# Two-layer decoder trunk on one core: scores a head further ahead, norm factors spread by matmuls, two tiles divided anew

## The chip, the core and the metric

The kernel runs on one core of a Trainium2 chip. The metric is the time of one execution on the device in microseconds (us); a version's time is the median of several executions. A difference under 0.2% (2.8 us here) is treated as no difference.

## The reference

`h` is 512 tokens by 1024 channels, all in float32. Two layers are computed, each an attention, a SwiGLU feed-forward part and a gated embedding:

```python
# layer 0: stick-breaking attention, 16 heads of 64
q, k, v = split(rms(h) @ sb_w_qkv)                 # 1024 -> 3 x 1024
z = q @ k.T * 64**-0.5
later = reverse_cumsum(where(strict, -softplus(z), 0)) - where(strict, -softplus(z), 0)
w = where(strict, exp(log_sigmoid(z) + later), 0)
h += (w @ v) @ sb_w_o
# layer 1: softmax attention with a forget bias, keys and values from the shared projection
kvf = rms(h, shared_norm_g) @ shared_w_kvf         # keys, values, 16 forget logits a token
f_cum = cumsum(log_sigmoid(kvf[..., 2048:] + b_f), over tokens)
h += softmax(rms(q) @ rms(k).T * 64**-0.5 + f_cum[q] - f_cum[k]) @ v @ fox_w_o
# every layer, then
h += (silu(rms(h) @ w_g) * (rms(h) @ w_u)) @ w_d   # 2816 wide
h += sigmoid(rms(h) @ ple_w_gate) * (p[i] @ ple_w_proj)
```

## The kernel before

`h` is held channels by tokens: 8 tiles `h0` to `h7` of 128 channels by 512 tokens. Every product keeps float32 accuracy by splitting both operands into a high part (`wh`, `bh`: rounded by ScalarE) and a rest (`wl`, `bl`: subtracted by VectorE), and by three matmuls, high by high, high by rest and rest by high. `dense` makes one 128 by 512 output tile so (three matmuls for each of 8 input tiles); `by_token` makes its output tokens by channels, with 256 columns a matmul. Weights come as units of 128 by 1024, in the order of use, into two buffers `raw` by DMAs on SP's queue; `load_unit` splits a unit into `wh` and `wl`, three units ahead of use.

The norms' row factors are not applied to `h` but after the product. `norm_sums` sums squares by four small matmuls (tile `ssq`) and makes the 4 columns `r` with a Newton iteration on VectorE. The factors are needed along the free dimension too, in tile `rb` (128 by 512, equal rows): `norm_spread` makes it by four matmuls against the identity into tile `pb` and a ScalarE copy, `norm_bounce` by writing `r` to DRAM (`row<-r`) and reading it back to all partitions (`rb<-row`), both on SP's queue.

An attention interleaves three streams by hand. `front(hd)` makes the scores of a head in three PSUM tiles `z` (512, 384 and 256+128 columns) and turns them into weights `w`: in layer 0 ScalarE takes two sigmoids `e` and `w`, VectorE runs a product scan over `e` (L630) and multiplies (L633). `back(hd)` turns `w` by TensorE transposes in three groups (`pt`, L682: 4, 4 and 2 blocks, two PSUM buffers in turn), splits each group into high and rest (`w3h`/`w3l`, `w2h`/`w2l`, `w1h`/`w1l`), multiplies them with the values into `po` (L690), and adds the two halves into `at` (ScalarE L710, VectorE L711). `fill` holds other work for TensorE between these steps: keys and queries of later pairs of heads (`qk`: `kr`, then `ke`/`kd` and `qd`, of which halves are copied across partitions by DMAs that GpSimd issues, L518), values, and part of the output product. `STEPS[layer]` is the order in which one head's steps are taken: "f" is a step of the next head's `front`, "g" one of this head's `back`, and the number says how many steps of `fill` follow. A scheduler then moves instructions within each engine's queue; every queue runs in order.

In layer 1 the queries and keys are made by token in groups of four heads (`group`), with a norm a head (L551 to L565, result `qn`), and turned by `expand` (tile `qt`, L586). At the start of the layer, `group(0, sums, gates)` makes the queries, calls `sums` (which calls `norm_sums` and `norm_bounce`), and the rest of `forget` (L474 on) needs `rb` for the forget logits `zf`, whose running sum goes through DRAM (`gdram`) to the tiles `gb` that the scores need.

The gated embedding at the end of each layer (in `ffn`) makes for each tile `n` a gate product `pg` (24 matmuls) and a projection `pp` (6), then `gate` computes `h += sigmoid(pg * rb) * pp`. Its last tile is done in two parts of 384 and 128 columns (`LASTS`).

Of the kernel before, what the change touches and what calls it, by code (L numbers as in the profile page):

```python
# [18 lines left out]
F32 = mybir.dt.float32  # L19
# [5 lines left out]
P = 128  # L25
# [4 lines left out]
NP = 8  # L30
EPS = 1e-6
EXPLN = "natural_log_exp_and_others"
LASTS = [(0, 384), (384, 128)]
FULL = [(0, 512)]


# [49 lines left out]
def trunk(ctx, tc, xT, pT, small, wf, wall, out, dump=None):  # L86
# [8 lines left out]


    sm = const.tile([P, NG], F32, name="sm")
    nc.sync.dma_start(sm, small)
    h = []
    for k in range(ND):  # L100
        h.append(res.tile([P, S], F32, name=f"h{k}", tag=f"h{k}"))
    ident = const.tile([P, P], F32, name="ident")
    make_identity(nc, ident)

# [21 lines left out]
        nc.vector.tensor_tensor(out, a, b.bitcast(F32), ALU.subtract)  # L126


    raws, units = {}, {}
    gains = {}  # L130
    state = {"unit": 0, "block": 0, "low": "vector"}
    NU = wall.shape[0]
# [5 lines left out]
    def load_unit(u):  # L138
# [5 lines left out]
        if u in gains:  # L144
            c0, nk = gains[u]
            n = 1024 // nk
            for k in range(nk):
                c, g = slice(k * n, (k + 1) * n), sm[:, c0 + k:c0 + k + 1]
                nc.scalar.activation(wh[:, c], raw[:, c], AF.Copy, scale=g)
                nc.vector.scalar_tensor_tensor(wl[:, c], raw[:, c], g, wh[:, c].bitcast(F32),  # L150
                                               ALU.mult, ALU.subtract)
        else:
            nc.scalar.copy(wh, raw)  # L153
            if state["low"] == "dma":

# [109 lines left out]
    def dense(*args):  # L265
        return run(dense_steps(*args))
# [8 lines left out]
    def ffn(layer, buf, g_next):  # L275
        last = layer == 1
        with tc.tile_pool(name=f"pf{layer}", bufs=8, space=PSUM, reuse_waits="tile") as ppool["d"], \
# [44 lines left out]
            dumph(f"h_ffn{layer}")  # L322

            px = [(ph[:, k, :], pl[:, k, :]) for k in range(2)]
            tiles = [(n, 0, S) for n in range(ND)]
            tiles[-1:] = [(ND - 1, c0, cn) for c0, cn in LASTS]

            def gate():
                n, c0, cn, pp, pg = waiting.pop(0)
                s = ft.tile([P, S], F32, name="s", tag="s")  # L330
                nc.vector.tensor_tensor(s[:, :cn], pg[:, :cn], rb[:, c0:c0 + cn], ALU.mult)
                nc.scalar.activation(s[:, :cn], s[:, :cn], AF.Sigmoid)
                nc.vector.tensor_tensor(s[:, :cn], s[:, :cn], pp[:, :cn], ALU.mult)
                grow(n, s, c0, cn)
                if last:
                    nc.sync.dma_start(out[:, n * S + c0:n * S + c0 + cn], h[n][:, c0:c0 + cn])
                else:
                    emit_x(n, 1 - buf, g_next, True, c0, cn)

            blocks = [take(10) for n in range(ND)]  # L340
            for i, (n, c0, cn) in enumerate(tiles):
                if i == 0:
                    pp = dense(blocks[n], px, c0, cn)
                pg = dense(blocks[n] + 2, xs, c0, cn)
                if i > 0:
                    pp = dense(blocks[n], px, c0, cn)
                waiting.append((n, c0, cn, pp, pg))
                if i == 0:
                    m, r = norm_sums()
                elif i == 1:  # L350
# [13 lines left out]
    def attention(layer, buf):  # L364
# [3 lines left out]
        with tc.tile_pool(name=f"pa{layer}", bufs=1, space=PSUM, reuse_waits="tile") as pa, \  # L368
# [12 lines left out]
            vq = {}  # L381
            tok = {}

            def by_token(xs, emit, halves=((0,), (1,))):

                b = take(16)
                for hs in halves:
                    pss = {t2: ppool["d"].tile([P, 2, 256], F32, name="psv", tag="d") for t2 in hs}
# [153 lines left out]
            def group(g, before=None, after=None):  # L542

                for what in "qk":
# [24 lines left out]
                    if what == "q" and before is not None:  # L569
# [2 lines left out]
                        before()  # L572
                        for a in held:
                            emit(*a)
                        run(after)
                    else:
                        yield from by_token(xs, emit)
                    if what == "q":
# [141 lines left out]
            else:  # L720
                def sums():
# [1 line left out]

                    tok["em"] = a1.tile([P, 4], F32, name="em")
                    nc.vector.tensor_scalar_mul(tok["em"], m, EPS)
                    tok["rb"] = norm_bounce(tok["r"])
                    next(gates)

                gates = forget()
# [11 lines left out]
                    grow(n, ps)  # L741
                    yield

            run(front(0))
            with (tc.manual_schedule(engines={mybir.EngineType.PE}) if PIN[layer] else nullcontext()):
                for hd in range(NH):
                    if hd == 2 * WO_SPLIT:
                        fill.add("wo", first_part())
                    if hd + 1 < NH:
                        fill.finish(f"{'p' if stick else 'e'}{(hd + 1) // 2}")  # L750
                        f = front(hd + 1)
                    else:
                        f = iter(())
                    if hd % 4 == 0:
# [36 lines left out]
    for k in range(ND):  # L791
        nc.sync.dma_start(h[k], xT[:, k * S:(k + 1) * S])
        if k in (0, 4):
            fetch(k // 4)
    for k in range(ND):
        emit_x(k, 0, G_ATTN[0], False)
        if k in (0, 4):
# [135 lines left out]
```

## Time and profile before

| | us |
|---|---|
| median of 3 executions (lowest, highest) | 1397.88 (1397.15, 1398.16) |
| the profiled execution: its own time | 1396.51 |
| the profiled execution: its span, first to last instruction | 1394.7 |
| TensorE busy in the span | 1359.7 (97%) |
| VectorE busy in the span | 807.2 (58%) |
| ScalarE busy in the span | 633.3 (45%) |

A share of busy time is an average over stages. Matmuls overlap: one of 512 columns is shown as some 0.39 us long while the next starts 0.227 us after it, so a wait of TensorE costs more than the gap that the profile shows. The stages, by the first and last instruction: loads 0 to 7, first values and keys 7 to 50, first attention's heads 50 to 283 (from the first score to the sums of squares), feed-forward part and embedding to 701, second attention to 985, the rest of layer 1 to 1394.7.

### The profile page before, as it was taken

The numbers are of one execution on the slowest core, as the hardware profiler recorded it, in microseconds if no ns is written. First come the engines' busy times: TensorE is split into PE (matmuls) and PEld (weight loads), VectorE is DVE, ScalarE is ACT, GpSimd is POOL, SyncE is SP. The second block draws the span as 40 slices with busy tenths as digits, with TensorE's granted clock in tenths as the row PEclk, the third lists the DMA queues.
The fourth block names the chain that finished last, engine by engine and source line by source line (L and its number), as shares of the span: only waits on it lengthen the run. The fifth ranks groups of instructions, "written<-read, shape, count | busy, mean of one in ns | idle before, by whom it ended". The sixth has DMA issues, their size and how long they took to land.

```text
span 1394.7 us, 18219 instructions
## 1 busy us (share of the span) xinstructions
PE 1359.7 (97%) x7108; PEld 1147.6 (82%) x7108; DVE 807.2 (58%) x1396; ACT 633.3 (45%) x1114; POOL 45.4 (3%) x96
## 2 busy tenths in 40 slices
PE   7999999999999999999969999999999999999999
PEld 7778877788888888888968999987888888888887
DVE  6788888844444443334847788778454444433335
ACT  5566666623332332222547888767333233322312
POOL 0110010000000000000001101100000000000000
PEclk9999999999999999999999999999999999999999
DMA  5332232333333333232254333332333332323323
GB/s 182 104 93 77 69 99 61 92 84 116 95 91 106 91 104 93 91 106 68 91 70 137 93 98 91 99 106 76 84 119 93 98 99 91 106 91 101 95 68 106
DMA packets 41958, 133.71 MB, mean 96 GB/s; under 512 B 7936, under 2 KB 8320, under 8 KB 41872
## 3 DMA queue, kind: packets, MB, share of 16 engines
q1 hardware_dynamic: 37488, 119.92, 29.8%
q0 software_dynamic: 4384, 12.62, 3.4%
q8 instruction: 56, 0.92, 0.3%
q14 instruction: 30, 0.25, 0.1%
HBM read 121.99 MB, written 2.14 MB: 89 GB/s over the span
## 4 chain that ended last, share of the span: by engine, by line
PE 83%; DVE 5%; ACT 5%; issue 4%; DMA 2%; POOL 0%; SPq 0%; DVEq 0%; POOLq 0%; ACTq 0%
PE ps L251 23%; PE ps L252 23%; PE ps L253 23%; PE psv L399 3%; PE psv L398 3%; PE psv L400 3%; PE po L690 2%; PE pt L682 2%; PE z L597 1%; DVE e L630 1%; PE z L598 1%; ACT ke L506 1%; DMA row<-r 1%; DVE w L633 1%; ACT qd L506 1%
## 5 line engine op out<-in xcount | busy, mean ns | idle before, releaser
L251 PE MATMUL ps<-bh,wh 128*128 128x512 f32 (+1 forms) x1232 | 483.7, 393 | 1.4 <-ACT bh L713 1.4
L252 PE MATMUL ps<-bl,wh 128*128 128x512 f32 (+1 forms) x1232 | 478.4, 388 | 0.0
L253 PE MATMUL ps<-bh,wl 128*128 128x512 f32 (+1 forms) x1232 | 478.1, 388 | 0.0
L153 ACT CAST wh<-raw 128x1024 fp32r<-128x1024 f32 x192 | 202.0, 1053 | 471.9 <-PE ps L252 414.6
L126 DVE TENSOR_TENSOR wl<-raw,wh 128x1024 fp32r<-128x1024 f32 x192 | 234.6, 1222 | 160.6 <-ACT wh L153 160.0
L253 PEld LDWEIGHTS ps<-bh,wl 128*128 128x128 f32 x1232 | 231.4, 188 | 46.6 <-DVE wl L126 0.2
L251 PEld LDWEIGHTS ps<-bh,wh 128*128 128x128 f32 x1232 | 231.8, 188 | 44.9 <-ACT bh L713 1.8
L252 PEld LDWEIGHTS ps<-bl,wh 128*128 128x128 f32 x1232 | 231.8, 188 | 43.6 <-DVE bl L126 0.4
L398 PE MATMUL psv<-wh,bh 128*128 128x256 f32 x512 | 151.4, 296 | 9.8 <-ACT wh L153 7.0
L399 PE MATMUL psv<-wl,bh 128*128 128x256 f32 x512 | 147.5, 288 | 0.5 <-DVE wl L126 0.5
L400 PE MATMUL psv<-wh,bl 128*128 128x256 f32 x512 | 147.4, 288 | 0.0
L398 PEld LDWEIGHTS psv<-wh,bh 128*128 128x128 f32 x512 | 99.5, 195 | 10.4 <-ACT wh L153 7.0
L294 DVE TENSOR_TENSOR s<-s,ps 128x512 f32<-128x512 f32 x44 | 30.3, 688 | 124.5 <-PE ps L253 124.3
L399 PEld LDWEIGHTS psv<-wl,bh 128*128 128x128 f32 x512 | 99.5, 194 | 1.7 <-DVE wl L126 0.8
L400 PEld LDWEIGHTS psv<-wh,bl 128*128 128x128 f32 x512 | 99.4, 194 | 0.1
L251 PE MATMUL ps<-eh,wh 128*128 128x512 f32 x224 | 87.1, 389 | 0.0
L252 PE MATMUL ps<-el,wh 128*128 128x512 f32 x224 | 87.1, 389 | 0.0
L253 PE MATMUL ps<-eh,wl 128*128 128x512 f32 x224 | 87.1, 389 | 0.0
L292 DVE TENSOR_TENSOR s<-ps,rb 128x512 f32<-128x512 f32 x44 | 30.2, 691 | 97.9 <-PE ps L253 79.9
L682 PE MATMUL pt<-ident,w 128*128 128x128 f32 x320 | 52.5, 275 | 6.4 <-DVE w3l L126 5.4
L630 DVE TENSOR_TENSOR_SCAN e<-e 128x512 f32<-128x512 f32 (+1 forms) x64 | 50.2, 812 | 3.2 <-ACT e L627 2.9
L682 PEld LDWEIGHTS pt<-ident,w 128*128 128x128 f32 x320 | 38.0, 140 | 16.7 <-DVE w3l L126 10.2
(142 smaller groups left out, 1567.1 us busy)
## 6 DMA issues: line engine op xcount, KB each, us to landing
raw<-in_w_dram SPq DMA_DIRECT2D x216, 512.0 KB, 3.6
kd<-ke POOLq DMA_DIRECT2D x32, 128.0 KB, 3.3
ke<-kd POOLq DMA_DIRECT2D x32, 128.0 KB, 4.2
gb<-gdram POOLq DMA_DIRECT2D x16, 256.0 KB, 3.7
h<-in_x_dram SPq DMA_DIRECT2D x8, 256.0 KB, 5.9
out_dram<-h SPq DMA_DIRECT2D x7, 256.0 KB, 2.0
rb<-row SPq DMA_DIRECT2D x5, 256.0 KB, 4.5
pf<-in_p_dram SPq DMA_DIRECT2D x2, 512.0 KB, 3.7
```

The costliest lines, as they stand in the source:

```text
L126: nc.vector.tensor_tensor(out, a, b.bitcast(F32), ALU.subtract)
L153: nc.scalar.copy(wh, raw)
L251: nc.tensor.matmul(ps, wh, xh, start=first, stop=False)
L252: nc.tensor.matmul(ps, wh, xl, start=False, stop=False)
L253: nc.tensor.matmul(ps, wl, xh, start=False, stop=last)
L292: nc.vector.tensor_tensor(s, g, rb, ALU.mult)
L294: nc.vector.tensor_tensor(s, s, u, ALU.mult)
L398: nc.tensor.matmul(ps[:, st], xh, wh, start=first, stop=False)
L399: nc.tensor.matmul(ps[:, st], xh, wl, start=False, stop=False)
L400: nc.tensor.matmul(ps[:, st], xl, wh, start=False, stop=lastk)
L630: nc.vector.tensor_tensor_scan(e[:, c:c + m], e[:, c:c + m], e[:, c:c + m], 1.0, ALU.mult, ALU.bypass)
L682: nc.tensor.transpose(pt[:, bi * P:(bi + 1) * P], blk(j, s), ident)
```

## The change

In layer 0, `front` runs two heads ahead of `back` instead of one (`LEAD`), with nine instead of six buffers for `w` and a new order of steps, in which the scores' three steps are spread between those of `back`. In layer 1's attention, `rb` is made by `norm_spread` within the first group's key product instead of by `norm_bounce`, and that product's first tile takes the PSUM bank of `qt` (tile `k0`). In both layers the last embedding tile keeps its gate product whole and divides only the projection, into halves of 256. The first weight unit is loaded and split as 256 and 768 columns, and `h0` is loaded first.

```diff
-LASTS = [(0, 384), (384, 128)]
+HALVES = [(0, 256), (256, 256)]
...
-    nc.sync.dma_start(sm, small)
+    nc.sync.dma_start(h[0], xT[:, :S])
+    raw0 = wpool.tile([P, 1024], F32, name="raw0", tag="raw", bufs=2)
+    nc.sync.dma_start(raw0[:, :256], wall[0, :, :256])
+    nc.sync.dma_start(sm, small)
+    nc.sync.dma_start(raw0[:, 256:], wall[0, :, 256:])
...
+        elif u == 0:
+            for c in (slice(0, 256), slice(256, 1024)):
+                nc.scalar.copy(wh[:, c], raw[:, c])
+                minus(wl[:, c], raw[:, c], wh[:, c])
...
             def gate():
-                n, c0, cn, pp, pg = waiting.pop(0)
+                n, pp, pg = waiting.pop(0)
                 s = ft.tile([P, S], F32, name="s", tag="s")
-                nc.vector.tensor_tensor(s[:, :cn], pg[:, :cn], rb[:, c0:c0 + cn], ALU.mult)
-                nc.scalar.activation(s[:, :cn], s[:, :cn], AF.Sigmoid)
-                nc.vector.tensor_tensor(s[:, :cn], s[:, :cn], pp[:, :cn], ALU.mult)
-                grow(n, s, c0, cn)
...
+                nc.vector.tensor_tensor(s, pg, rb, ALU.mult)
+                nc.scalar.activation(s, s, AF.Sigmoid)
+                for c0, ps in pp:
+                    c = slice(c0, c0 + S // len(pp))
+                    nc.vector.tensor_tensor(s[:, c], s[:, c], ps[:, :S // len(pp)], ALU.mult)
+                    nc.vector.tensor_tensor(h[n][:, c], h[n][:, c], s[:, c], ALU.add)
+                    if last:
+                        nc.sync.dma_start(out[:, n * S + c0:n * S + c0 + S // len(pp)], h[n][:, c])
...
+                elif n:
+                    pp = [(c0, dense(blocks[n], px, c0, cn)) for c0, cn in HALVES]
...
+                    elif after is not None:
+                        steps = by_token(xs, emit, first_bank=lambda: pz.tile(
+                            [P, S], F32, name="k0", tag="n", bufs=1))
+                        for _ in range(ND - 1):
+                            yield next(steps)
+                        tok["rb"] = norm_spread(tok["r"], pz, "z")
                         run(after)
+                        yield from steps
...
-                    tok["rb"] = norm_bounce(tok["r"])
...
-            run(front(0))
+            for hd in range(LEAD[layer]):
+                run(front(hd))
...
-                    if hd + 1 < NH:
-                        fill.finish(f"{'p' if stick else 'e'}{(hd + 1) // 2}")
-                        f = front(hd + 1)
+                    nxt = hd + LEAD[layer]
+                    if nxt < NH:
+                        fill.finish(f"{'p' if stick else 'e'}{nxt // 2}")
+                        f = front(nxt)
...
-WB = (6, 4)
+WB = (9, 4)
+LEAD = (2, 1)
...
-    [("f", 1), ("f", 1), ("f", 2), ("g", 2), ("g", 1), ("g", 1), ("g", 1), ("g", 2), ("g", 1)],
+    [("g", 1), ("f", 1), ("g", 1), ("g", 1), ("f", 2), ("g", 1), ("g", 2), ("f", 1), ("g", 2)],
```

What this does to the queues is seen in the order of the built instructions. First TensorE in a head in the middle of layer 0's attention, from the first transposes `pt` to the third group (the dense matmuls `ps` between them cut). Before:

```order
L682 MATMUL pt<-ident,w 128x128 x4
L251 MATMUL ps<-bh_104,wh_1706 128x512
L252 MATMUL ps<-bl_106,wh_1706 128x512
L253 MATMUL ps<-bh_104,wl_1707 128x512
...
L682 MATMUL pt<-ident,w 128x128 x4
...
L690 MATMUL po<-w3h,v 128x512
...
L682 MATMUL pt<-ident,w 128x128 x2
```

And in the changed kernel (line numbers there are its own: L682 is now L707, L597 is L622):

```order
L707 MATMUL pt<-ident,w 128x128 x4
...
L622 MATMUL z<-ke,qd 128x512
L623 MATMUL z<-kd,qd 128x512
...
L707 MATMUL pt<-ident,w 128x128 x4
...
L715 MATMUL po<-w3h,v 128x512
...
L622 MATMUL z<-ke,qd 128x384
L623 MATMUL z<-kd,qd 128x384
...
L707 MATMUL pt<-ident,w 128x128 x2
```

Between the first and the third group, which use the same PSUM buffer, stood 12 dense matmuls, one group of transposes and one product; now 18 dense matmuls and two score tiles stand there beside them. Before, all scores of the next head stood ahead of the first group.

Second, VectorE at the start of the heads of layer 0's attention, from the second head's middle score tile on (`kr` is the next pair's keys, `kd` their rest). Before:

```order
L630 SCALAR_TENSOR_TENSOR e<-e 128x384
L633 TENSOR_TENSOR w<-w,e 128x383
L126 TENSOR_TENSOR w3l<-pt,w3h 128x512
L630 SCALAR_TENSOR_TENSOR e<-e 128x256
L630 SCALAR_TENSOR_TENSOR e<-e 128x128
L633 TENSOR_TENSOR w<-w,e 128x255
L633 TENSOR_TENSOR w<-w,e 128x127
L126 TENSOR_TENSOR w2l<-pt,w2h 128x512
L535 TENSOR_TENSOR kr<-ps,rb 128x512
L126 TENSOR_TENSOR w1l<-pt,w1h 128x256
L126 TENSOR_TENSOR wl_695<-raw_692,wh_694 128x1024
L508 SCALAR_TENSOR_TENSOR kd<-kr,ke 64x512 x2
```

And in the changed kernel:

```order
L655 SCALAR_TENSOR_TENSOR e<-e 128x384
L658 TENSOR_TENSOR w<-w,e 128x383
L553 TENSOR_TENSOR kr<-ps,rb 128x512
L655 SCALAR_TENSOR_TENSOR e<-e 128x256
L655 SCALAR_TENSOR_TENSOR e<-e 128x128
L658 TENSOR_TENSOR w<-w,e 128x255
L658 TENSOR_TENSOR w<-w,e 128x127
L130 TENSOR_TENSOR wl_676<-raw_673,wh_675 128x1024
L526 SCALAR_TENSOR_TENSOR kd<-kr,ke 64x512 x2
```

`kd` and what follows from it now come ahead of the first head's `w3l`, `w2l` and `w1l`. On TensorE the third head's first score, which needs `kd`, has moved forward: 44 dense matmuls stand between the first head's first score and it, where 47 and all products of the first head stood.

Third, ScalarE in layer 1 behind the forget logits' product `fps`. Before:

```order
L471 COPY zf<-fps 16x512
L551 ACTIVATE sqn<-psv 128x512
L477 ACTIVATE ef<-zf 16x512
L560 ACTIVATE r_5844<-mm 128x8
L478 ACTIVATE ef<-ef 16x512
```

And in the changed kernel:

```order
L489 COPY zf<-fps 16x512
L247 COPY rb<-pb 128x512
L569 ACTIVATE sqn<-k_5725 128x512
L495 ACTIVATE ef<-zf 16x512
L496 ACTIVATE ef<-ef 16x512
```

The copy of `pb` is new here. On TensorE the four matmuls into `pb` stand behind the first 42 of the 48 matmuls into `k0`, and on SP's queue the two DMAs of `norm_bounce` are gone.

## Rows read from the trace of the kernel before

**Rows 1.** Busy time by stretch: stretch, its length, busy us (instructions) by engine, clock, DMA.
```profile
0.00:7.05 7.05, 0.00 (x1) 0.01 (x1) 0.99 (x4) 3.57 (x4) 1.77 (x12) 1.00 0.67 196
...
50.40:70.70 20.30, 18.09 (x90) 13.50 (x91) 17.87 (x28) 13.51 (x26) 2.07 (x4) 1.00 0.32 80
70.70:239.10 168.40, 164.04 (x942) 133.92 (x943) 141.97 (x225) 110.99 (x213) 12.36 (x24) 1.00 0.28 79
239.10:283.10 44.00, 43.12 (x205) 34.42 (x204) 35.15 (x51) 26.18 (x43) 0.00 (x0) 1.00 0.31 94
...
700.90:744.30 43.40, 30.10 (x223) 27.42 (x222) 21.95 (x68) 17.07 (x42) 3.71 (x7) 0.88 0.53 91
```

**Rows 2.** TensorE's groups by line and shape, 70.7 to 239.1 us.
```profile
L251 PE MATMUL ps<-bh,wh 128*128 128x512 f32 x120 | 51.9, 433 | 0.0
...
L682 PE MATMUL pt<-ident,w 128*128 128x128 f32 x129 | 20.9, 275 | 3.9 <-DVE w3l L126 3.7
```

**Rows 3.** VectorE in order of time, a head in the middle of the first attention.
```profile
141.12 1.39 DVE L508 SCALAR_TENSOR_TENSOR qd<-ps,qd 64x512 fp32r<-64x512 f32 x2
142.54 0.69 DVE L126 TENSOR_TENSOR w3l<-pt,w3h 128x512 fp32r<-128x512 f32 x1
```

**Rows 4.** VectorE's groups by line, 70.7 to 239.1 us.
```profile
L711 DVE TENSOR_TENSOR at<-at,po 64x512 f32<-64x512 f32 x12 | 8.2, 686 | 16.9 <-ACT at L710 16.8
```

**Rows 5.** VectorE in order of time, at the start of the first attention's heads.
```profile
51.95 1.23 DVE L630 TENSOR_TENSOR_SCAN e<-e 128x512 f32<-128x512 f32 x1 [0.89 <-ACT e L627]
...
65.13 1.40 DVE L508 SCALAR_TENSOR_TENSOR kd<-kr,ke 64x512 fp32r<-64x512 f32 x2
```

**Rows 6.** The chain that ended last, there: start us, us, what.
```profile
66.10 4.48 DMA ke<-kd
```

**Rows 7.** The chain that ended last, at the start of the second attention.
```profile
709.67 10.60 DMA row<-r
720.29 4.48 DMA rb<-row
```

**Rows 8.** TensorE's waits, 700 to 745 us: total us, times, longest us.
```profile
PE qt L586 <- DVE qn L565: 10.5, 1, 10.5
PE psv L398 <- DVE u L212: 2.4, 1, 2.4
```

**Rows 9.** VectorE in order of time, when the factors have come back from DRAM.
```profile
724.87 0.68 DVE L474 TENSOR_TENSOR zf<-zf,rb 16x512 f32<-16x512 f32 x1 [14.83 <-DMA rb<-row]
```

**Rows 10.** Busy time by stretch, shorter stretches (columns as in Rows 1).
```profile
8.90:13.81 4.91, 4.91 (x25) 4.91 (x24) 4.75 (x10) 4.91 (x9) 0.00 (x0) 1.00 0.84 325
14.24:23.00 8.76, 8.76 (x76) 8.76 (x75) 7.23 (x10) 4.97 (x8) 0.00 (x0) 1.00 0.53 149
...
727.36:737.60 10.24, 2.86 (x14) 2.86 (x15) 8.06 (x21) 5.21 (x14) 1.62 (x3) 0.50 0.27 70
...
1376.69:1382.82 6.13, 6.13 (x29) 5.07 (x28) 2.83 (x5) 1.07 (x2) 0.00 (x0) 1.00 0.21 79
1382.82:1388.04 5.22, 5.22 (x31) 5.22 (x30) 1.94 (x3) 0.44 (x2) 0.00 (x0) 1.00 0.15 53
1388.04:1391.34 3.30, 3.30 (x31) 3.30 (x30) 1.41 (x3) 0.42 (x2) 0.00 (x0) 1.00 0.17 60
```

**Rows 11.** The chain that ended last, in the first 9 us.
```profile
1.65 4.28 DMA raw<-in_w_dram
...
5.95 1.05 ACT wh L153
...
7.03 1.24 DVE wl L126
```

**Rows 12.** ScalarE in order of time, its first work.
```profile
4.59 0.72 ACT L190 ACTIVATE bh<-h,sm 128x512 fp32r<-128x512 f32 x1 [2.58 <-DMA h<-in_x_dram]
```

**Rows 13.** All engines in order of time, the last work.
```profile
1391.61 0.29 DVE L333 TENSOR_TENSOR s<-s,ps 128x128 f32<-128x128 f32 x1 [0.45 <-ACT s L332]
...
1392.25 0.33 SPq L336 DMA_DIRECT2D out_dram<-h  x1
```

More of the change, by code (lines that the diff above doesn't have):

```diff
@@ L126, in minus @@
         nc.vector.tensor_tensor(out, a, b.bitcast(F32), ALU.subtract)
-    raws, units = {}, {}
+    raws, units = {0: raw0}, {}
     gains = {}
@@ L324, in ffn @@
             px = [(ph[:, k, :], pl[:, k, :]) for k in range(2)]
-            tiles = [(n, 0, S) for n in range(ND)]
-            tiles[-1:] = [(ND - 1, c0, cn) for c0, cn in LASTS]
             def gate():
-                n, c0, cn, pp, pg = waiting.pop(0)
+                n, pp, pg = waiting.pop(0)
                 s = ft.tile([P, S], F32, name="s", tag="s")
-                nc.vector.tensor_tensor(s[:, :cn], pg[:, :cn], rb[:, c0:c0 + cn], ALU.mult)
-                nc.scalar.activation(s[:, :cn], s[:, :cn], AF.Sigmoid)
-                nc.vector.tensor_tensor(s[:, :cn], s[:, :cn], pp[:, :cn], ALU.mult)
-                grow(n, s, c0, cn)
[L335 to L338, printed above, removed]
@@ L340, in ffn @@
-            blocks = [take(10) for n in range(ND)]
[L341 to L348, printed above, removed]
+                nc.vector.tensor_tensor(s, pg, rb, ALU.mult)
+                nc.scalar.activation(s, s, AF.Sigmoid)
@@ new lines, in gate @@
+                for c0, ps in pp:
[4 more added lines that the diff above has]
+                        nc.sync.dma_start(out[:, n * S + c0:n * S + c0 + S // len(pp)], h[n][:, c])
+                    else:
+                        emit_x(n, 1 - buf, g_next, True, c0, S // len(pp))
@@ L349, in ffn @@
+            blocks = [take(10) for n in range(ND)]
+            for n in range(ND):
+                if n == 0:
+                    pp = [(0, dense(blocks[n], px))]
+                pg = dense(blocks[n] + 2, xs)
+                if 0 < n < ND - 1:
+                    pp = [(0, dense(blocks[n], px))]
+                elif n:
+                    pp = [(c0, dense(blocks[n], px, c0, cn)) for c0, cn in HALVES]
+                waiting.append((n, pp, pg))
+                if n == 0:
                     m, r = norm_sums()
-                elif i == 1:
+                elif n == 1:
@@ L382, in attention, with by_token @@
             tok = {}
-            def by_token(xs, emit, halves=((0,), (1,))):
+            def by_token(xs, emit, halves=((0,), (1,)), first_bank=None):
                 b = take(16)
                 for hs in halves:
-                    pss = {t2: ppool["d"].tile([P, 2, 256], F32, name="psv", tag="d") for t2 in hs}
+                    pss = {}
+                    for t2 in hs:
+                        if t2 == 0 and first_bank:
+                            ps = first_bank().rearrange("p (s c) -> p s c", s=2)
+                        else:
+                            ps = ppool["d"].tile([P, 2, 256], F32, name="psv", tag="d")
+                        pss[t2] = ps
                     for k in range(ND):
@@ L790, in trunk @@
     table("sigmoid_and_others")
-    for k in range(ND):
+    for k in range(1, ND):
         nc.sync.dma_start(h[k], xT[:, k * S:(k + 1) * S])
-        if k in (0, 4):
-            fetch(k // 4)
+        if k == 4:
+            fetch(1)
     for k in range(ND):
```

## The prediction

> **What bounds the kernel now.** I read first the busy time by stretch: in each stretch, its length less TensorE's busy time is TensorE's idle time. In the whole span it idles only 35 us (1394.7 less 1359.7). Of this 7 lie before its first matmul, 2.2 and 4.4 in the first attention's heads, 0.9 behind them, and 13.3 in the 43 us at the start of the second attention [rows 1]. Elsewhere matmul follows matmul, so the kernel is bound by TensorE, and a change gains only where it shortens one of these gaps or TensorE's own work. Then I read who ends the gaps: the groups of TensorE and VectorE in the first attention, the chain and the waits in the second, and the clock.
>
> **First attention.** Idle time understates here, since a matmul is drawn longer than the spacing to the next. I priced the 942 matmuls of 70.7 to 239.1 us (13 heads) by their undisturbed spacing: 360 of 512 columns (three lines of 120 [rows 2]) at 0.227 are 81.7, 129 transposes [rows 2] at 0.11 are 14.2, 192 of by_token at 0.12 are 23.0, scores 21.0, products 16.7: 156.6 in all. The stretch took 168.4, so 11.8 us are stalls, 0.9 a head. The same count gives 5.8 of stalls ahead of 81.9 us (three first head steps) and 2.2 in the last head: some 17.9 from the first score to the sums of squares. The largest group of stalls is the transposes' wait for VectorE's `w3l` [rows 2]: the third group reuses the first one's PSUM buffer, and `w3l`, which reads it, stands behind `qd` and the scans of the next head [rows 3]. For that VectorE is 84% busy [rows 1], yet waits 16.9 us in 12 places for `at`, the end of a head's `back` [rows 4]. It gets its work in bursts.
>
> The new order spreads the scores. By the order of instructions, 18 dense matmuls and two score tiles now lie between the first and third group instead of 12: 5.9 us of TensorE's work by the spacings above instead of 3.6, for one ScalarE copy and one VectorE subtraction of 0.69 [rows 3] with what queues ahead. Weights `w` are ready a head earlier. What is late next is VectorE itself: 142 us busy over 13 heads [rows 1] are 10.9 a head against 12.05 of TensorE's work, 91%. I take 0.35 a head for the stalls that stay (bounds 0.1 and the old 0.9).
>
> The start of the heads gains little. Reckoned from the first score T (50.4, first scan 1.55 later [rows 5]), VectorE now runs two heads' scans (before, these ended, with `w3l` between, about 11 us behind the first), then a unit's `wl`, then `kd`; without idle its first `kd` is ready at T + 13.9. The copy of `kd` to `ke` across partitions then takes 4.5 from issue to landing [rows 6], so the third head's score cannot start before T + 18.7; TensorE, with 44 dense matmuls, two heads' scores and 8 transposes, is there at T + 14. That is a stall of about 4.7 in place of 5.8 (bounds 3.5 and 6.5). At the end the supply of fill work runs out earlier: two heads without scores and with little fill, so I put 3.2 there instead of 2.2. Sum: 17.9 less (4.7 + 13 x 0.35 + 3.2) is **5.5; I take 6** (bounds: -2, with no stall removed in the middle and 6.5 at the start, and +10).
>
> **Second attention.** The chain at its start goes through DRAM: `row<-r` 10.6, `rb<-row` 4.5 [rows 7], and VectorE stands for 14.8 us at `zf`, which needs `rb` [rows 9]. The normalized keys `qn` stand behind `zf` in VectorE's queue, so TensorE's transposes `qt` wait 10.5 us, after 2.4 us for a free bank [rows 8]. In the gap the granted clock falls to half for 10.2 us, with 2.9 us of matmuls in them [rows 10], which costs 1.4.
>
> Now `r` (ready at 709.67 [rows 7]) goes into four matmuls behind 42 of the 48 of `k0`. `k0` has a bank of its own, so the 2.4 us wait goes and these start at 706.0; 42 x 0.12 + 4 x 0.11 is 711.5, a ScalarE copy of 0.6 makes `rb`, and `zf` starts at about 712.3 instead of 724.87: 12.6 earlier, and `qn`, `gdram` and `gb` with it. TensorE's own work from 706.0 to the first score is 23.1, which ends at 729.1; the chain (744.4 less 12.6, less up to 1.4 of slow clock) gives 730.4 to 731.8. So the chain still ends last, by 1 to 3 us of short waits for `qn` and `kd`, too short to show the clock an idle engine as long as the present one. First score 12.6 to 14.0 earlier, 1.0 more of TensorE's work left behind it (products that the order has moved): **12** (bounds 8.5, with 4 us more of GpSimd's copies and of VectorE's queue, and 13.5). The two DMAs less on SP's queue also free the weight load that stood between them; nothing waits for it.
>
> **Last embedding tile.** Spacings: 30 matmuls of 384 columns in 5.22 are 0.174, 30 of 128 in 3.30 are 0.110, of 512 columns 0.227 [rows 10]. Before: 30 x (0.174 + 0.110) = 8.5. Now: 24 x 0.227 + 12 x 0.12 = 6.9. In layer 0, where the next product follows without a wait, that is **1.65** (bounds 1.5, 1.7). [...]
>
> At the very end the gate's VectorE work counts instead. Before, the last multiply starts 0.4 after the last matmul's start, and 3.1 later the span ends [rows 13]: counted from the tile's first matmul, 8.4 + 0.4 + 3.1 = 11.9. Now the multiply by `rb` and the sigmoid are 512 wide. They start 0.4 behind the gate product's last matmul (5.2 from the first) and take some 0.7 each [rows 3, 12]; then come four VectorE passes of 0.42 (an estimate between 0.29 at 128 columns [rows 13] and 0.69 at 512), and from the last store's issue to the end 2.45 [rows 13] and 0.2 for its double size: 5.2 + 0.4 + 1.4 + 1.7 + 2.65 = 11.4, while TensorE is done at 6.9. That is **0.5** (bounds 0.2, 1.2).
>
> **Start.** The first matmul waits for the whole first unit: landed at 5.93, ScalarE 1.05, and the second for VectorE's 1.24 [rows 11]. Now `h0` is first in the queue, 0.45 earlier than its 4.55 [rows 12]; behind it ScalarE has a square of 0.6, a quarter of the unit's cast (0.3) and `bh` 0.72 [rows 12]: first matmul at about 5.8, `wl` and `bl` in time. The first 12 matmuls end near 8.6 instead of 10.6. [...] I take **1.6** (bounds 0.8, 2.2; the later inputs `h1` to `h7` land as before and are needed 2 us sooner, which their order allows).
>
> **Sum.** 6 + 12 + 1.65 + 0.5 + 1.6 = 21.8 from the profiled execution's 1396.5: 1374.7. The median lies 1.4 above that execution, so **1376.1**.
>
> **Rivals.** (1) VectorE is the bound of the first attention: the stalls move from `w3l` to `at`, `kd` or the scans. For it speaks its 91%; against it the 16.9 us of waiting that spread scores can fill. Gain there 0 to -2: 1382 to 1384. (2) In the second attention the next thing late, GpSimd's copies `kd`/`ke` or the second `qn`, takes half of the 12.6; for it speaks that `qt` and these copies stand on the chain already; against it that their rows behind `zf` just shift: 1382. (3) Slower: VectorE's fixed order puts a later head's scan ahead of `w3l` or `at` where TensorE needs it, and TensorE waits in every head. The rest gains 15.8, so it decides from 33.7 us of stalls in place of 17.9, 2.1 a head over 16 heads; at 2.3 a head, 36.8 in all, the time is 1401. Against it speak the 5.9 us of distance, and that the 0.9 a head of today hold all waits together. (4) The spread scores feed all engines and nearly no stall stays: 1370.
>
> **Numbers.** The forecast 0.70 (its own range 1371 to 1381), (1) 0.15, (2) 0.06, (3) 0.03, (4) 0.06. The range 1369 to 1385 leaves out (3) and the ends of the bounds. A measurement of this kernel tells 0.2%, 2.8 us: faster 0.95, same 0.02, slower 0.03.
>
> **What would show it.** First matmul near 5.8; no long VectorE wait for `rb` at the start of the second attention, TensorE's longest wait there under 2 us and no half clock; its wait for `w3l` near 0; in the first attention one wait of 4 to 5 us for `ke<-kd` at the third head; from there 12.4 us a head. The forecast is wrong if VectorE is over 95% busy in these heads, if the wait for `qt` stays over 5 us, or if a new wait recurs with every head.

## The result and the profile after

The changed kernel takes 1374.67 us (median of 4 executions, 1373.89 to 1375.25) against 1397.52 for the kernel before, timed beside it on the same chip: a ratio of 0.9837 (95% interval 0.982 to 0.9854). The forecast was 1376.1. The profiled execution spans 1372.1 us, 22.6 less than before.

Where these 22.6 lie, cut at the same matmuls in both traces (first score, sums of squares `ssq`; gains are taken before rounding):

| stretch | before | after | gain | forecast |
|---|---|---|---|---|
| start to first score | 50.4 | 49.5 | 0.8 | 1.6 |
| first attention, first score to `ssq` | 232.7 | 226.0 | 6.8 | 6 |
| feed-forward part, layer 0 | 355.9 | 355.9 | 0 | 0 |
| embedding, layer 0 | 61.9 | 60.1 | 1.7 | 1.65 |
| second attention, `ssq` to `ssq` | 284.2 | 271.5 | 12.7 | 12 |
| feed-forward part, layer 1 | 355.9 | 355.9 | 0 | 0 |
| embedding, layer 1, to the end | 53.7 | 53.1 | 0.6 | 0.5 |

Busy time by stretch of the changed kernel: its start, its first attention in three parts (start, middle and end of the heads) and the start of its second attention. It answers to [rows 1], with the same columns; the cuts at 69.98 and 231.00 do not lie at the same matmuls as 70.70 and 239.10 there, but the middle holds nearly the same work (940 and 942 matmuls, 225 instructions of VectorE in both):

```profile
0.00:5.30 5.30, 0.00 (x0) 0.00 (x0) 0.56 (x4) 2.83 (x4) 1.76 (x12) 1.00 0.52 150
49.54:69.98 20.44, 17.40 (x83) 13.37 (x84) 17.88 (x27) 13.58 (x26) 2.07 (x4) 0.94 0.36 104
69.98:231.00 161.02, 161.02 (x940) 135.66 (x938) 143.40 (x225) 111.30 (x210) 12.40 (x24) 1.00 0.30 82
231.00:275.53 44.53, 44.22 (x215) 35.80 (x215) 35.87 (x53) 27.79 (x46) 0.00 (x0) 1.00 0.27 83
691.58:721.60 30.02, 28.54 (x224) 26.12 (x222) 21.15 (x64) 16.54 (x41) 3.70 (x7) 1.00 0.42 120
```

TensorE's idle time in the middle is nil, where it was 4.4; at the start of the heads it has grown from 2.2 to 3.0, and the mean clock there is 0.94. The second attention's start is 13.4 shorter, and its idle time is 1.5 instead of 13.3. VectorE does the same work in the middle heads and is 89% busy (143.40 of 161.02).

TensorE's waits of the changed kernel, first in 70 to 265 us (the first row, which answers to the second of [rows 2]), then at the start of the second attention, 691 to 735 us (three rows, to [rows 8]):

```profile
PE po L715 <- DVE at L736: 0.2, 1, 0.2
...
PE qt L611 <- DVE mm L573: 0.8, 1, 0.8
PE z L622 <- DMA ke<-kd: 0.6, 1, 0.6
PE qt L611 <- DVE kd L526: 0.2, 1, 0.2
```

The wait for `w3l` is gone, and so is the 10.5 us one for `qt`. Rows of the changed kernel in order of time: the first matmul; a wait at the second value product; the third head's first score; a head in the middle of the first attention; `zf` in the second attention (against [rows 9]); the last gate (against [rows 13]):

```profile
5.30 0.58 PE L416 MATMUL psv<-wh,bh 128*128 128x256 f32 x1 [5.30 <-ACT bh L199]
...
29.66 0.36 PE L416 MATMUL psv<-wh,bh 128*128 128x256 f32 x1 [0.86 <-DVE v L437]
...
62.72 1.40 DVE L526 SCALAR_TENSOR_TENSOR kd<-kr,ke 64x512 fp32r<-64x512 f32 x2
...
67.38 0.48 PE L622 MATMUL z<-ke,qd 128*128 128x512 f32 x1 [3.04 <-DMA ke<-kd]
...
141.48 0.60 PE L707 MATMUL pt<-ident,w 128*128 128x128 f32 x4
...
145.71 0.69 DVE L130 TENSOR_TENSOR w3l<-pt,w3h 128x512 fp32r<-128x512 f32 x1
...
147.84 0.38 PE L707 MATMUL pt<-ident,w 128*128 128x128 f32 x2
...
702.84 0.68 DVE L492 TENSOR_TENSOR zf<-zf,rb 16x512 f32<-16x512 f32 x1 [3.47 <-ACT rb L247]
...
1367.10 0.63 ACT L339 ACTIVATE s<-s 128x512 f32<-128x512 f32 x1 [6.17 <-DVE s L338]
1367.48 0.28 PE L262 MATMUL ps<-ph,wl 128*128 128x256 f32 x1
1367.76 0.75 DVE L342 TENSOR_TENSOR s<-s,ps 128x256 f32<-128x256 f32 x2 [0.70 <-PE ps L262]
1368.43 0.75 DVE L343 TENSOR_TENSOR h<-h,s 128x256 f32<-128x256 f32 x2
```

`zf` starts 11.3 us behind the sums of squares (691.58), where it started 24.0 behind them (724.87 less 700.90). In the middle head `w3l` starts 4.2 us behind the first transposes, which is late, but the third group comes 6.4 behind them and finds its buffer free. The new thing is at the third head. Busy time by stretch during its wait and behind it:

```profile
63.95:67.36 3.41, 0.40 (x2) 0.01 (x1) 3.29 (x5) 0.87 (x2) 0.77 (x2) 1.00 0.91 243
67.70:71.11 3.41, 3.41 (x11) 2.33 (x10) 2.26 (x3) 1.33 (x3) 0.00 (x0) 0.50 0.27 106
```

TensorE waits 3.0 us for the copy of `kd` into `ke`, and then runs 3.4 us at half clock (0.50 in the second row). The wait was forecast, the clock was not.

### The profile page after: what moved, and what is told of

Its sections match the earlier page's. It is cut to its first block, busy times and chain, and to the rows that moved or that the text cites. A ratio compares the mean times of both kernels' runs of the same rounds, so it can differ in the third digit from the quotient of the medians.

```text
span 1372.1 us, 18133 instructions
## 1 busy us (share of the span) xinstructions
PE 1353.2 (99%) x7068; PEld 1145.6 (83%) x7068; DVE 808.9 (59%) x1395; ACT 634.1 (46%) x1114; POOL 45.3 (3%) x96
## 4 chain that ended last, share of the span: by engine, by line
PE 85%; issue 7%; ACT 4%; DVE 2%; DMA 1%; POOL 0%; SPq 0%; DVEq 0%; POOLq 0%; ACTq 0%
PE ps L260 23%; PE ps L261 23%; PE ps L262 23%; PE po L715 3%; PE psv L418 3%; PE psv L416 3%; PE psv L417 3%; PE pt L707 2%; PE z L622 2%; PE z L623 1%; ACT w L670 1%; DMA raw<-in_w_dram 1%; ACT w L674 1%; ACT qd L524 1%; DMA ke<-kd 1%
## 5 line engine op out<-in xcount | busy, mean ns | idle before, releaser
L260 PE MATMUL ps<-bh,wh 128*128 128x512 f32 x1216 | 481.6, 396 | 1.4 <-ACT bh L738 1.4
L262 PE MATMUL ps<-bh,wl 128*128 128x512 f32 x1216 | 475.4, 391 | 0.0
L261 PE MATMUL ps<-bl,wh 128*128 128x512 f32 x1216 | 475.0, 391 | 0.0
L130 DVE TENSOR_TENSOR wl<-raw,wh 128x1024 fp32r<-128x1024 f32 (+1 forms) x193 | 234.8, 1217 | 170.8 <-ACT wh L162 164.1
L416 PE MATMUL psv<-wh,bh 128*128 128x256 f32 x496 | 146.7, 296 | 6.4 <-ACT bh L199 5.6
L418 PE MATMUL psv<-wh,bl 128*128 128x256 f32 x496 | 143.0, 288 | 0.1
L417 PE MATMUL psv<-wl,bh 128*128 128x256 f32 x496 | 142.8, 288 | 0.0
L416 PEld LDWEIGHTS psv<-wh,bh 128*128 128x128 f32 x496 | 96.1, 194 | 7.0 <-ACT bh L199 5.9
L417 PEld LDWEIGHTS psv<-wl,bh 128*128 128x128 f32 x496 | 96.1, 194 | 1.0
L707 PE MATMUL pt<-ident,w 128*128 128x128 f32 x320 | 52.4, 273 | 0.0
L622 PE MATMUL z<-ke,qd 128*128 128x256 f32 (+2 forms) x128 | 46.9, 367 | 4.3 <-DMA ke<-kd 3.6
```

Of the source, the lines that this page charges most:

```text
L260: nc.tensor.matmul(ps, wh, xh, start=first, stop=False)
L261: nc.tensor.matmul(ps, wh, xl, start=False, stop=False)
L262: nc.tensor.matmul(ps, wl, xh, start=False, stop=last)
L416: nc.tensor.matmul(ps[:, st], xh, wh, start=first, stop=False)
L417: nc.tensor.matmul(ps[:, st], xh, wl, start=False, stop=False)
L418: nc.tensor.matmul(ps[:, st], xl, wh, start=False, stop=lastk)
```

## The experiments

In the first table below, the stalls in the first attention are the length of a stretch less TensorE's work in it by the prediction's spacings: twelve middle heads are 147.25; the three head steps ahead of them are 24.5 with the scores two heads ahead and 25.7 with one; the last is 43.1 and 41.8. Four kernels (fill moved, the factors through DRAM, no bank, the last tile as before) were timed on another chip, where the kernel before took 1398.5; every ratio is to the kernel before on the same chip. Medians less than 2.8 us apart count as no difference here; what is said of such kernels rests on one trace each.

**What took the waits for `w3l` away.** Three kernels take the lead and the order apart. The first has the old order with the new lead:

```diff
-    [("g", 1), ("f", 1), ("g", 1), ("g", 1), ("f", 2), ("g", 1), ("g", 2), ("f", 1), ("g", 2)],
+    [("f", 1), ("f", 1), ("f", 2), ("g", 2), ("g", 1), ("g", 1), ("g", 1), ("g", 2), ("g", 1)],
```

> The changed kernel with the old order of a head's steps (the three score steps of a head first, then the steps of back), two heads ahead as in the change. Nothing is left out. Theory A (the gain in the middle heads comes from the distance between the transpose groups: 18 dense matmuls and two score tiles instead of 12): the distance is back to 12 dense matmuls, so TensorE's waits for w3l come back, 0.7 to 0.9 us a head instead of 0.3, the twelve middle heads lose 5 to 7 us and the time is 1380 to 1382 against 1374.7. Theory B (the gain comes from the weights w being ready a head earlier, wherever the scores stand): the time stays at 1374 to 1376 and the waits for w3l stay under 0.35 us a head.

The second has the new order with the old lead:

```diff
-LEAD = (2, 1)
+LEAD = (1, 1)
```

> The changed kernel with the new order of steps, but the scores run one head ahead as before. Nothing is left out. Theory A (the spread order needs the second head of lead): the last score tile of the next head now stands only two steps of fill and one step of back ahead of the transposes of its weights; ScalarE's two sigmoids, two scans and two multiplies lie between them, some 4 us for about 1 us of TensorE's work, so TensorE waits for w in every head, 2 to 3 us, and the time is 1400 to 1420. Theory B (the order of steps alone gives the gain and the lead is not needed): the time is 1374 to 1377, with waits of some 0.3 us a head.

The third has the old lead and the old sequence of steps, but moves fill work to the transposes:

```diff
-LEAD = (2, 1)
+LEAD = (1, 1)
-    [("g", 1), ("f", 1), ("g", 1), ("g", 1), ("f", 2), ("g", 1), ("g", 2), ("f", 1), ("g", 2)],
+    [("f", 1), ("f", 1), ("f", 1), ("g", 2), ("g", 2), ("g", 2), ("g", 1), ("g", 1), ("g", 1)],
```

> The changed kernel with scores one head ahead and with the old sequence of steps (the three score steps of a head first), but the fill work moved from the end of a head to its transposes, so that in two heads together 57 dense matmuls instead of 36 stand between a head's first and third transpose group. Nothing is left out. Theory A (the distance in TensorE's work between the groups is what took the waits for w3l away): few waits for w3l stay, 0.5 us a head or less, 1374 to 1379. Theory B (it is the spreading of the scores, so that VectorE's scans do not stand in a row ahead of w3l): the waits for w3l or for w stay, 0.8 us a head or more, 1381 or more.

Measured (stalls at the start, in the middle and at the end of the heads; mean times over the twelve middle heads from the first transposes to the end of `w3l` and to the third group):

| kernel | time | first score to `ssq` | stalls | `w3l` ends | third group |
|---|---|---|---|---|---|
| before | 1397.5 | 232.7 | 5.8, 9.9, 2.3 | 4.06 | 4.25 |
| new lead, old order | 1386.95 | 238.5 | 5.6, 13.9, 4.3 | 4.37 | 4.67 |
| old lead, new order | 1375.88 | 227.1 | 5.2, 6.9, 0.3 | 3.39 | 6.54 |
| old lead, old sequence, fill moved | 1377.37 | 228.5 | 5.6, 6.4, 1.8 | 4.47 | 5.55 |
| the change | 1374.67 | 226.0 | 5.7, 3.6, 1.9 | 3.29 | 6.18 |

Not all that this count leaves in the middle is waiting. In the changed kernel it leaves 3.6 us, but TensorE is never idle there, its waits from 70 to 265 us are 0.2 in all, and no matmul of these heads starts more than 0.32 us behind the one ahead of it (1.22 in the kernel before). In all eight profiles that have the change's heads these twelve take 150.7 to 150.8 us. So the count is about 3.6 us too low; some 2 us of that are the dense matmuls, which start 0.233 us apart there (median) and not 0.227. The matmuls are the same in every row, so about the same 3.6 is in each, and differences between rows stand. Without it, the stalls in the middle are some 6.3 us before, 10.3, 3.3 and 2.8 in the three kernels, and about none in the change.

With the new lead and the old order TensorE's waits, 70 to 265 us, and a head in order of time read:

```profile
PE pt L707 <- DVE w3l L130: 7.2, 11, 1.0
```

```profile
137.72 0.60 PE L707 MATMUL pt<-ident,w 128*128 128x128 f32 x4
...
138.37 1.00 DVE L655 TENSOR_TENSOR_SCAN e<-e 128x256 f32<-128x256 f32 x2
139.28 0.60 DVE L658 TENSOR_TENSOR w<-w,e 128x255 f32<-128x255 f32 x2
139.80 1.22 DVE L130 TENSOR_TENSOR wl<-raw,wh 128x1024 fp32r<-128x1024 f32 x1
141.05 1.39 DVE L526 SCALAR_TENSOR_TENSOR qd<-ps,qd 64x512 fp32r<-64x512 f32 x2
142.47 0.69 DVE L130 TENSOR_TENSOR w3l<-pt,w3h 128x512 fp32r<-128x512 f32 x1
...
143.22 0.44 PE L707 MATMUL pt<-ident,w 128*128 128x128 f32 x2 [0.99 <-DVE w3l L130]
```

Here `w3l` starts 4.75 us behind the first transposes, hardly later than the 4.2 in the changed kernel's head above; but the third group is due after 4.5 and waits. So Theory A, the distance, held in kind, but not in size: the twelve heads lose 10.3 us to the change where 5 to 7 were expected, and the time is 1386.95 where it said 1380 to 1382. The lead alone removes nothing (the attention is 5.8 us longer than before).

Moving fill work between the groups, with `w3l` no earlier than before (4.47 against 4.06), takes 3.5 of the 9.9 us of middle stalls away, and the time lies in Theory A's range. Its count of matmuls was off: by the trace 18 dense matmuls, or as much work of `by_token`, stand between the groups, 36 in two heads, where 24 stood before. Nor do the scores all stay in a row, since in every second head two score tiles stand between the groups too. In the heads without them `w3l` ends 3.4 to 4.4 us behind the first transposes and the third group comes after 5.3 to 5.4, without a wait, so the dense matmuls alone are enough. All three kernels keep the nine buffers for `w`, which were not tried alone; in the trace before no engine waits for a buffer of `w` between 70 and 240 us, so six did not hold the old order up. In the two kernels with the old lead the waits that are left are no longer one kind. New order, then moved fill, 70 to 265 us:

```profile
PE pt L707 <- DVE w L658: 2.6, 7, 0.5
PE po L715 <- DVE w1l L130: 0.2, 1, 0.2
```

```profile
PE pt L707 <- DVE w3l L130: 0.9, 1, 0.9
PE po L715 <- ACT w1h L708: 0.6, 1, 0.6
PE z L622 <- ACT w L652: 0.5, 3, 0.2
PE po L715 <- DVE w1l L130: 0.3, 2, 0.2
```

For the new order with the old lead, Theory A was wrong by 24 us or more, and the time is in Theory B's range: Theory A saw the last scores just ahead of the transposes of their weights, but between them stand 2.7 us of fill and products, nearly enough, and TensorE waits for `w` at most 0.5. The second head of lead is worth only 3.3 us in the middle (6.9 less 3.6), of which it gives 2.1 back at the start and the end (7.6 against 5.5); the two medians are 1.2 apart.

**The wait at the third head.** This kernel makes the second pair's keys and queries between the first two heads:

```diff
             for hd in range(LEAD[layer]):
+                if hd == 1:
+                    fill.finish("p1")
                 run(front(hd))
```

> The changed kernel with the keys and queries of the second pair of heads (kr, ke, kd, qd) made between the first and the second head's scores, not behind both. Nothing is left out. Theory A (the third head's score waits 3.0 us for the copy of kd because kr and kd stand behind two heads' scans on VectorE, and the half clock of 3.4 us behind that wait comes from the wait): the wait for ke<-kd and the half clock between 60 and 75 us both go; 3 to 5 us less, 1370 to 1372. Theory B (VectorE is full there, so the wait only moves to the first heads' weights or subtractions): the wait for ke<-kd goes, a wait of like length for w or w3l stands in its place, the time is within 1.5 us of 1374.7. Theory C (the wait goes but the clock falls for another reason): about 3 us less, and a stretch at half clock stays there.

1371.14 us (ratio to before 0.9806, 0.9791 to 0.982). `kd` is done before the second head's scans, the wait and the half clock are gone, as Theory A had it, and of the 5.7 us of stalls at the start 2.2 stay. VectorE's rows, and the two waits of TensorE that are left between 50 and 75 us:

```profile
55.98 0.69 DVE L553 TENSOR_TENSOR kr<-ps,rb 128x512 f32<-128x512 f32 x1
56.59 1.21 DVE L130 TENSOR_TENSOR wl<-raw,wh 128x1024 fp32r<-128x1024 f32 x1
57.73 1.40 DVE L526 SCALAR_TENSOR_TENSOR kd<-kr,ke 64x512 fp32r<-64x512 f32 x2
...
63.12 0.39 PE L622 MATMUL z<-ke,qd 128*128 128x256 f32 x1 [0.46 <-ACT w L652]
...
68.73 0.44 PE L707 MATMUL pt<-ident,w 128*128 128x128 f32 x2 [0.39 <-DVE w3l L130]
```

**The second attention's start, in two halves.** First the factors through DRAM, with the bank `k0` kept:

```diff
-                        tok["rb"] = norm_spread(tok["r"], pz, "z")
                         run(after)
...
                     nc.vector.tensor_scalar_mul(tok["em"], m, EPS)
+                    tok["rb"] = norm_bounce(tok["r"])
```

> The changed kernel with the norm factors of the second attention's start going through DRAM again, while the key product keeps its own bank k0. Nothing is left out. Theory A (the chain through DRAM sets the start, the bank only moves a wait): VectorE waits some 15 us for rb again, TensorE waits 10 to 13 us for qt, the clock falls to half behind it, and the time is 11 to 13 us above the changed kernel's 1374.7, at 1386 to 1388. Theory B (the bank is most of the gain, since TensorE could run on during the trip through DRAM): 1 to 4 us above, 1376 to 1379.

Then the factors by matmuls, without the bank:

```diff
-                        steps = by_token(xs, emit, first_bank=lambda: pz.tile(
-                            [P, S], F32, name="k0", tag="n", bufs=1))
+                        steps = by_token(xs, emit)
```

> The changed kernel with the norm factors spread by matmuls, but the first half of the key product in the common pool of banks as before, not in k0. Nothing is left out. Theory A (the wait of 2.4 us for a free bank, seen before the change, comes back ahead of the chain, and rb with it): TensorE waits 2 to 2.4 us near 707 us, rb and the first score come as much later, 1376 to 1377.5. Theory B (the chain behind rb has slack for it): a wait of 2.4 us is seen but the first score comes at 721.6 as with the change, 1374.7 within 0.7.

| `rb` | `k0` | time | ratio to before | `ssq` to first score | `ssq` to `ssq` |
|---|---|---|---|---|---|
| DRAM | shared (before) | 1397.5 | | 43.4 | 284.2 |
| DRAM | own | 1384.93 | 0.9903 | 38.6 | 280.4 |
| matmuls | shared | 1377.33 | 0.9848 | 31.4 | 273.1 |
| matmuls | own (the change) | 1374.67 | 0.9837 | 30.0 | 271.5 |

Through DRAM `zf` waits again, 21.9 us behind the sums of squares, TensorE waits 8.4 for `qt`, and 10.2 us of half clock stand behind it; `zf` in order of time, the wait, and the stretch:

```profile
714.75 0.68 DVE L492 TENSOR_TENSOR zf<-zf,rb 16x512 f32<-16x512 f32 x1 [10.08 <-DMA rb<-row]
```

```profile
PE qt L610 <- DVE qn L583: 8.4, 1, 8.4
```

```profile
711.93:722.17 10.24, 4.73 (x22) 4.73 (x23) 6.72 (x16) 6.07 (x16) 0.00 (x0) 0.50 0.37 101
```

Without the bank the wait for it comes back, 1.7 us, and 1.4 of it reach the first score:

```profile
PE psv L416 <- DVE u L221: 1.7, 1, 1.7
PE qt L610 <- DVE qn L583: 0.7, 1, 0.7
```

So the chain is most of it: 8.9 of 12.7 us by `ssq` to `ssq`. Theory A was right in kind and too large: it had 10 to 13 us for the wait for `qt`, some 15 for `rb` (10.1 in the row above) and 1386 to 1388 for the time. The median is 10.3 above the change's, but 1.9 us of that are the first attention, where this profile's half clock lasted 6.8 us, and by the ratios it is 9.2.

The bank is 1.6 beside the chain. The time without it, 1377.33, fits Theory A in part by luck: of the 3.4 us by which its span exceeds the change's, 1.1 lie in the two embedding stretches, where a weight unit comes late. The bank alone, with DRAM, gave 3.9: a matter of one trace each, and more than either theory had for it.

**The last embedding tile as before.** The diff is that of the change, backwards.

> The changed kernel with the last embedding tile of both layers divided as before, 384 and 128 columns of gate product and projection. Nothing is left out. Theory A (TensorE's spacing of 128-column matmuls, 0.110 us, prices it): layer 0 takes 1.7 us more, from 60.2 back to 61.9 between its two rows of sums of squares, the end of the span 0.5 more, together 2.2: 1376.2 to 1377.5. [...] Beside it: this kernel has the start of the first attention unchanged, so a wait of some 3 us for ke<-kd near 64 us is to be seen again; if such a wait makes the clock fall to half, that is seen here too, and if not, the fall has another cause.

1376.79 us (ratio 0.9846, against the change's 0.9837). Layer 0's embedding takes 62.3 instead of 60.1, the last stretch 54.7 instead of 53.1. Of this, 0.3 and 0.85 come from a late weight unit in the middle of the stretch, where the next matmul starts 0.52 and 1.08 us behind the one ahead of it, not 0.23. Other kernels here show this at the same place, ahead of the tile that the edit touches; the wait in the last stretch reads

```profile
PE ps L262 <- DVE wl L130: 0.7, 1, 0.7
```

That leaves 1.8 and 0.8, or 1.6 and 0.6 against the longest such stretches without the wait (60.4 and 53.3), where 1.7 and 0.5 were expected. The time fits Theory A in part by luck: the late units add to it, and the first attention is 1.4 us shorter than the change's, since its clock stayed whole at the third head behind a wait of 3.2 (512-column matmuls 0.23 us apart behind it, where the change has them 0.43 apart).

**The start.** The second half of the second value product takes a score bank (`by_token` gets a parameter `last_bank` for it, made as `first_bank` is in the change):

```diff
-                v1 = by_token(xs, keep_values(value_tile(1), r))
+                v1 = by_token(xs, keep_values(value_tile(1), r), last_bank=lambda: pz.tile(
+                    [P, S], F32, name="v1b", tag="z"))
```

> The changed kernel with the second half of the second value product written into a score bank of PSUM, so that it does not wait for a bank that VectorE still reads. Nothing is left out. Theory A (of the 1.75 us that the earlier first matmul gave, this wait of 0.86 us at 28.5 us gave 0.9 back): the wait goes, the first score comes at 48.6 instead of 49.5, 0.9 us less in span. Theory B (the score bank is then late for the first score, or the next product waits instead): the wait moves behind 28.5 us and the first score stays at 49.5.

1373.16 us (0.9821, 0.9804 to 0.9837). The wait is gone, and the first score comes at 49.0. The size is about half of Theory A's 0.9. In the other kernels, whose instructions up to the first score are those of the change, this wait was 0.2 to 0.9 (0.33 before the change) and the first score came between 48.9 and 49.9, while the clock rose at a different moment in each, from 8.8 to 15.0 us. That moment is read from the spacing of the 256-column matmuls, 0.21 us ahead of it and 0.12 behind; in the kernel before they are 0.21 apart in the half clock of the second attention too (735.44 to 737.36 us), and 0.12 behind it. Beside a profile with the same moment the gain is 0.4 (49.03 against 49.42 in the kernel with the new lead and the old order, both risen at 14.5 by that spacing). The first attention of this profile is 1.2 us shorter too, but for another reason: its clock stayed whole at the third head.

**Together, and the change once more.** The last kernel has the keys first, the score bank, and the last gate's multiply and sigmoid in halves, in both layers (the diff shows the third edit alone):

```diff
-                nc.vector.tensor_tensor(s, pg, rb, ALU.mult)
-                nc.scalar.activation(s, s, AF.Sigmoid)
+                for c0, ps in pp:
+                    c = slice(c0, c0 + S // len(pp))
+                    nc.vector.tensor_tensor(s[:, c], pg[:, c], rb[:, c], ALU.mult)
+                    nc.scalar.activation(s[:, c], s[:, c], AF.Sigmoid)
```

> The changed kernel with three edits on top: the second pair's keys between the first two heads' scores, the second value product's second half in a score bank, and the very last gate computed in halves of 256 columns. Nothing is left out. If the gains lie at three separate places they add: 3.5 us from the keys (1371.14 against 1374.67), 0.5 to 0.9 at the second value product, 0.5 at the end (the multiply by rb and the sigmoid of the first half take 0.4 us less each), so 1369.5 to 1370.5. The rival: the edits at the start overlap, since the wait for the keys swallows what comes earlier ahead of it; then 1371 within 0.7.

> The changed kernel itself once more, beside the combined one on the same chip. If a wait of some 3 us for ke<-kd is by itself what makes the clock fall, half clock is seen again behind 67 us and the second head's length is 12.3 us; if the fall needs something else, which differs from execution to execution, the clock may stay whole and that head takes 10.7 us. The time 1374.7 within 1.5.

The combined kernel takes 1368.95 us (0.9794, 0.978 to 0.9809), the change beside it 1374.89 (0.9835): 5.9 less, where 4.2 to 5.2 were expected. Its median is the lowest, but only 2.2 below that of the keys alone. By stretch against the repeat, the start is 1.2 shorter, the first attention 4.4 and the last stretch 0.6, so the edits add; of the 1.2, only some 0.55 are the bank's, by the profile whose clock rose about as early (48.35, its matmuls drawn at the short 0.38 us from 8.70 on, against 48.90, from 8.86 on, with the factors through DRAM). Its last stretch is 52.8 (53.4 in the change beside it): the sigmoid of the first half lets VectorE's multiply start while TensorE has two matmuls to go, where it started 0.28 behind the last one's start:

```profile
1362.43 0.75 ACT L341 ACTIVATE s<-s 128x256 f32<-128x256 f32 x2 [5.90 <-DVE s L340]
...
1362.85 0.28 PE L260 MATMUL ps<-ph,wh 128*128 128x256 f32 x1
1362.88 0.42 DVE L344 TENSOR_TENSOR s<-s,ps 128x256 f32<-128x256 f32 x1 [0.15 <-ACT s L341]
```

In the repeat the wait for `ke<-kd` was 4.0 us, and 3.4 us of half clock stood behind it again; from the third to the fourth head's first score it took 12.3.

## Why the prediction was right

**Second attention (12, measured 12.7).** Right in mechanism and size. `zf` came 12.7 us earlier against the sums of squares (12.6 forecast), the first score 13.4 (12.6 to 14.0), TensorE has three short waits of 1.5 in all (1 to 3), the half clock is gone, and the work left behind the first score cost 0.7 (1.0). Rival (2), that GpSimd's copies or the second `qn` take half of it, is refuted.

**First attention (6, measured 6.8).** The step that carried it held: the third transpose group now comes 6.2 us behind the first (5.9 forecast), later than `w3l`. The term "0.35 a head for the stalls that stay" fits only as a number: the count leaves 0.30 a head, but that is work priced too low and not waiting, as shown under the table of the three kernels. The old 0.9 a head has the same 0.3 in it, so the difference, which is the gain, was right. In the prediction's own words, what came in the middle is rival (4), nearly no stall; its 1370 took that 0.3 a head, too, for time to be gained. Rival (1) is refuted there, since VectorE at 89% keeps up. The second reason that stood beside it, weights ready a head earlier, is a smaller one: order without lead gives 5.6 of the 6.8 us, lead without order loses 5.8. Rival (3), a wait in every head, is nearly what the lead does under the old order (11 waits for `w3l` from 70 to 265 us). The "12.4 us a head" came out at 12.6, because its 12.05 of work was a mean over 13 heads of which the first is short. At the end of the heads 3.2 of stalls were forecast, 1.9 came by the same count.

**Start of the heads (stall 4.7, measured 5.7, and 6.6 in the repeat).** The place and the cause were right, VectorE's two heads of scans ahead of `kd`. The wait was forecast at 4 to 5 us and was 3.0 (4.0 in the repeat). What was missing is the clock: the prediction looked for a fall only in the second attention. Its cost is seen from the third to the fourth head's first score: 12.3 us with 3.4 us of half clock, 10.7 to 10.8 without, in kernels whose start is the same. In the two profiles without the fall the stall is 4.3 and 4.6, so for them the 4.7 was right.

**Start (1.6, measured 0.8).** The first matmul came at 5.3 (5.8 forecast), the first sums of squares 1.7 earlier, but the first score only 0.8. The step that failed is that the later work would move up whole. Some 0.5 of the difference is VectorE's reading of `v`, which holds a bank: 0.86 in this profile against 0.33 before; the rest is open. Nor is the 1.7 all the change's: by the spacing of the 256-column matmuls the clock rose at 13.1 us here and at 14.0 before. What an earlier or a later rise would give of the 1.6 was the author's estimate, and no run shows it: over the kernels with the same start the gain is 0.5 to 1.5.

**Last tile (1.65 and 0.5, measured 1.7 and 0.6).** Right, by the spacings of the rows.

That the sum came out so near (21.8 forecast, 22.6 in the spans) is in part luck: 0.8 too much at the start stood against 0.8 and 0.7 too little in the two attentions.

Rival (4)'s time, 1370, was within reach, but needed the keys' place changed too: 1371.14 with that alone, 1368.95 with all three later edits.

## What to carry to other kernels

When two engines pass a buffer back and forth and the slow one's work comes in bursts, count how much work the waiting engine has between its two uses of that buffer; more distance there can take the wait away even if the other engine gets no faster (with fill moved, some 6.3 us of middle stalls became 2.8, with `w3l` done after 4.47 us instead of 4.06). Running a producer further ahead can move its burst to the start: look there for what the burst now stands in front of (here the wait for `ke<-kd` went from 0.6 to 3.0 us). Undo a change's parts one at a time before crediting the part that gave it its name; here the order did most of what the lead was named for.

## What the runs showed of the hardware

Waits of TensorE much shorter than the 10.5 us one of before were followed by half clock. At the third head's score, waits of 3.0, 3.7, 3.9, 4.0 and 4.05 us came with 3.4 us of it behind them (6.8 at the one of 3.9), with 512-column matmuls 0.43 us apart. Waits of 3.2 us (the last tile as before) and 3.5 us (the score bank) were followed by none, with these matmuls 0.23 apart, and neither were waits under 1 us in these stretches. The score bank's wait, and the 3.4 us behind it at whole clock, against the rows of the change at 67.38 and 67.70:

```profile
67.35 0.47 PE L625 MATMUL z<-ke,qd 128*128 128x512 f32 x1 [3.48 <-DMA ke<-kd]
...
67.60:71.01 3.41, 3.41 (x19) 2.48 (x18) 2.08 (x4) 2.33 (x4) 0.00 (x0) 1.00 0.18 68
```

So the wait's length alone does not decide between 3.0 and 3.7 us. The moment of the clock's rise at the start varies too, 13.1 us in the change and 13.9 in its repeat by the spacing of the 256-column matmuls. Why the fall at the third head came in some profiles and not in others is not shown by any run here.
